# A decoder layer on one core: the FFN's out-projection as seven block products, with sums of operands formed on the fly

## The chip, the cores and the metric

One Trainium2 chip; the program runs on one core. The metric is the device time of one execution in microseconds (us), lower is better. A time is the median of several executions; beside it stands one profiled execution with its trace. The engines are called by the profile's names: PE (TensorE, matrix products), PEld (its weight loads), DVE (VectorE), ACT (ScalarE), POOL (GpSimd) and SP (SyncE, which only issues DMA transfers here).

## The reference

One layer over 1024 tokens of width 1024, all in fp32 (DEPTH is 1, so the sparse-attention branch is never reached):

```
def swiglu(x, w_in, w_out):
    a, b = jnp.split(x @ w_in, 2, axis=-1)
    return (jax.nn.silu(a) * b) @ w_out

h = x
h = h + stick_breaking_attention(rms_norm(h, norm_mix), w_in, w_out)   # 16 heads of 64
h = h + swiglu(rms_norm(h, norm_ffn), ffn_w_in, ffn_w_out)             # inner width 2816
gate = sigmoid(rms_norm(h, norm_ple) @ ple_w_gate)
h = h + gate * (p @ ple_w_proj)                                        # p: 1024 x 256
return rms_norm(h, final_norm)
```

## The kernel before

**Precision.** Each fp32 operand is split into a high part (a cast to fp32r, by ACT) and a low part (operand minus high part, by DVE or POOL). A product of two operands is then three matmuls: high by high, high by low, low by high (`mm3`, L126 to L129). Every matmul spoken of here has a 128x128 weight tile and 512 columns.

**Layout.** Tensors lie transposed: features on the 128 partitions, tokens along the free dimension. Width 1024 is 8 tiles (KT), the inner width 2816 is 22 tiles (NFF), and the tokens are taken in two halves of 512 (h).

**Stages.** Start (the first norm's split of x, its square sums, first Q and K products), attention with its projections (heads in pairs, 8 pairs), the embedding projection `p @ ple_w_proj` in the midst of that (stored to memory as `ple`, for the end), attention's out-projection, the FFN's in-projection, the FFN's out-projection, the gate with the final norm. Up to the FFN a scheduler orders the instructions; from the in-projection on, each engine runs in the order in which the code is written.

**FFN in-projection.** For each of the 22 inner tiles the 2x2-block product is computed with seven block products in place of eight (products P1 to P7 by Winograd's variant of Strassen's scheme; sums of weight blocks are formed by DVE, split by ACT and DVE or POOL). The SwiGLU result of tile k goes to memory as `act_d[k][h]`. The last tile's scalings are kept back as `rest_0` and `rest_1`, four DVE operations and one of ACT each, and are called inside the out-projection.

**FFN out-projection.** For h in 0, 1 and for k in 0 to 21: load `act_d[k][h]` (L618, 256 KB) and split it (`act_split`; ACT L626, DVE L627), load weight tile `w_fo[k]` (512 KB) and split it (`w_split`; ACT L106, DVE L108), then 8 output tiles m, three matmuls each, into 8 PSUM banks. That is 2 x 22 x 8 x 3 = 1056 matmuls. The last two k are done per m, so that the banks finish one by one; `residual` (L939) then adds h from memory. In the second half `parts3(m, 0)` splits the finished first half for the gate (ACT L944 `gh`, DVE L945 `gl`, ACT L950 square, and a sum of squares on POOL or DVE, L952). Five gate weights are split between k = 3 and k = 18 (`WGK`).

**Start.** Zeros for the unused halves of K's tiles (`KLS`) are written by POOL from a tile `zero` that POOL has set itself; the tile is also the source of ACT's `pad`.

**Embedding projection.** Each 128x512 block is copied from PSUM by ACT to a tile `plt` (three buffers in rotation, tag `qf`) and stored, 16 stores of 256 KB.

Of the kernel before, what the change touches and what calls it, by code (L numbers as in the profile page):

```python
# [40 lines left out]
def tile_trunk(ctx: ExitStack, tc: tile.TileContext, xT, pT, gains, ident, w_qkv, w_o, w_fi, w_fo, w_g, w_p, outT):  # L41
# [22 lines left out]
    for m in MORD:  # L64
        order.append((w_o[m], KT))
    n_fi = len(order)
    for h in range(2):
        for k in range(NFF):
            order.append((w_fo[k], KT, k == NFF - 1))
            if h == 1 and k in WGK:  # L70
                order.append((w_g[WGK.index(k)], KT, True))
    for m in range(len(WGK), KT):
        order.append((w_g[m], KT, m < 6))

    N1 = 3 * NPAIR + 2
    raws, parts, loaded = {}, {}, set()
# [19 lines left out]
    def w_split(k):  # L96
        if k < lim[0] and k in raws:
            n = order[k][1]
            t = raws.pop(k)
            if len(order[k]) > 2 and order[k][2]:  # L100
                hi = xp.tile([P, T], F32R, name=f"whi{k}", tag="X").rearrange("p (k m) -> p k m", k=KT)
                lo = xp.tile([P, T], F32R, name=f"wlo{k}", tag="X").rearrange("p (k m) -> p k m", k=KT)
            else:
                hi = wp.tile([P, KT, P], F32R, name=f"whi{k}", tag="whi", bufs=2)
                lo = wp.tile([P, KT, P], F32R, name=f"wlo{k}", tag="wlo", bufs=2)
            nc.scalar.copy(hi[:, :n, :], t[:, :n, :])  # L106
            eng = nc.gpsimd if k < N1 or n_fi <= k < n_fi + 2 or k >= len(order) - 3 else nc.vector
# [61 lines left out]
    with ExitStack() as c1:  # L169
# [77 lines left out]
        for kt in range(KT):  # L247
# [240 lines left out]
        def ple_steps():  # L488
# [118 lines left out]
    def tmp(name):  # L607
        return pt.tile([P, 512], F32, name=name, tag="t")

    ring[:] = [0, ctx.enter_context(tc.tile_pool(name="pr", bufs=2, reuse_waits="tile"))]  # L610

    tc_manual = tc.manual_schedule()
    acts = {}
    araw = {}

    def act_dma(i):
        if i < 2 * NFF and i not in araw and i not in acts:
            h, k = divmod(i, NFF)  # L618
            araw[i] = tmp("araw")
            nc.sync.dma_start(araw[i], act_d[k][h])  # L620

    def act_split(i):
        if i < 2 * NFF and i not in acts:
            t = araw.pop(i)
            a = duo(xp, f"act{i}", "X", None)
            nc.scalar.copy(a[:, 0, :], t)  # L626
            nc.vector.tensor_tensor(a[:, 1, :], t, f(a[:, 0, :]), op=ALU.subtract)  # L627
            acts[i] = a

    with ExitStack() as c2:  # L630
        p2 = c2.enter_context(tc.tile_pool(name="p2", bufs=1, reuse_waits="tile"))

        def add(out, x, y):
            nc.vector.tensor_tensor(out, x, y, op=ALU.add)  # L634
# [208 lines left out]
        for k in range(NFF):  # L843
            w = wc
            wc, todo = fi_prep(k + 1)
            fi_load(k + 2)
            if k >= NFF - 2:
                for i in range(2):
                    w_load(n_fi + 2 * (k + 2 - NFF) + i)
                act_dma(k + 2 - NFF)  # L850
            ps1 = prod(w["A11"], "B11")
            q1 = tmp("q1")
            nc.scalar.copy(q1, ps1)
# [41 lines left out]
            todo[4]()  # L895
            if 0 < k < NFF - 1:
                glu(k, 0, q1, u2)
            if k == NFF - 1:
                act_dma(2)
            ps3 = prod(w["S4"], "B22")  # L900
            if k == 0:
                for h in range(2):
# [20 lines left out]
            glu(NFF - 1, 1, u4, c22)  # L923

        rests = [rest_0, rest_1]


    p3 = ctx.enter_context(tc.tile_pool(name="p3", bufs=1, reuse_waits="tile"))
    hres = [p3.tile([P, T], F32, name=f"h{m}") for m in range(KT)]
    hh = [p3.tile([P, T], F32R, name=f"gh{m}") for m in range(KT)]  # L930
    hl = [p3.tile([P, T], F32R, name=f"gl{m}") for m in range(KT)]
# [6 lines left out]
    def residual(m, h, ps, t):  # L938
        nc.vector.tensor_tensor(hres[m][:, HS[h]], ps, t, op=ALU.add)  # L939

    def parts3(m, h):
        hs = HS[h]
        g = gn[:, 2, m:m + 1]
        nc.scalar.activation(hh[m][:, hs], hres[m][:, hs], AF.Copy, scale=g)  # L944
        nc.vector.scalar_tensor_tensor(hl[m][:, hs], hres[m][:, hs], g, f(hh[m][:, hs]), op0=ALU.mult, op1=ALU.subtract)  # L945
        if m == 0:
            nc.scalar.activation(acc3[:, hs], hres[m][:, hs], AF.Square)
        else:
            s = tmp("sq")
            nc.scalar.activation(s, hres[m][:, hs], AF.Square)  # L950
            eng = nc.vector if h and m % 2 else nc.gpsimd
            eng.tensor_tensor(acc3[:, hs], acc3[:, hs], s, op=ALU.add)  # L952

    y3 = None
    for h in range(2):
        pm = [None] * KT
        tail = []
        for k in range(NFF):
            i = h * NFF + k
            act_dma(i)  # L960
            act_split(i)
            act_dma(i + 1)
            act_dma(i + 2)
            wh, wl = w_next()
            if h == 1 and 2 <= k < 10:
                parts3(k - 2, 0)
            act_split(i + 1)
            a = acts.pop(i)
            if h == 1 and k in WGK:
                wg.append(w_next())  # L970
            if k < NFF - 2:
                for m in range(KT):
                    if k == 0:
                        pm[m] = mb()
                    mm3(pm[m], wh[:, m, :], wl[:, m, :], a[:, 0, :], a[:, 1, :], k == 0, False)
            else:
                tail.append((wh, wl, a))
            if k and rests:
                rests.pop(0)()
        res = []  # L980
        for m in range(KT):
            t = tmp("h2")
            nc.sync.dma_start(t, h2_d[m][h])
            res.append(t)
        for m in range(KT):
            for q, (wh, wl, a) in enumerate(tail):
                mm3(pm[m], wh[:, m, :], wl[:, m, :], a[:, 0, :], a[:, 1, :], False, q == 1)
            residual(m, h, pm[m], res[m])


    acc4 = row("acc4")
# [50 lines left out]
    for ri, (c0, n) in enumerate(ranges):  # L1042
# [3 lines left out]
        for m in range(KT):  # L1046
# [81 lines left out]
```

## Time and profile before

| what | value |
|---|---|
| median of 3 runs | 1380.06 us (1379.49 to 1381.41) |
| profiled execution: its own time | 1380.04 us |
| profiled execution: span of the trace | 1378.3 us |
| granted TensorE clock, mean | 0.996 |
| PE busy | 1353.9 us (98%) |
| DVE busy | 1004.1 us (73%) |
| ACT busy | 607.6 us (44%) |
| POOL busy | 408.3 us (30%) |

The span runs from the first to the last instruction in the trace; the execution's own time is 1.7 us longer. Busy shares are means over stages that are limited by different things. A matmul of 512 columns shows as 0.39 us, but the next begins 0.23 us later: matmuls overlap, and their rate is read from their starts.

### The profile page before, as it was taken

The numbers are of one execution on the slowest core, as the hardware profiler recorded it, in microseconds if no ns is written. First come the engines' busy times: TensorE is split into PE (matmuls) and PEld (weight loads), VectorE is DVE, ScalarE is ACT, GpSimd is POOL, SyncE is SP. The second block draws the span as 40 slices with busy tenths as digits, with TensorE's granted clock in tenths as the row PEclk, the third lists the DMA queues.
The fourth block names the chain that finished last, engine by engine and source line by source line (L and its number), as shares of the span: only waits on it lengthen the run. The fifth ranks groups of instructions, "written<-read, shape, count | busy, mean of one in ns | idle before, by whom it ended". The sixth has DMA issues, their size and how long they took to land. (4 is left out here: it accounts for less than half of the span.)

```text
span 1378.3 us, 17601 instructions
## 1 busy us (share of the span) xinstructions
PE 1353.9 (98%) x6620; PEld 1133.0 (82%) x6620; DVE 1004.1 (73%) x1305; ACT 607.6 (44%) x1082; POOL 408.3 (30%) x280
## 2 busy tenths in 40 slices
PE   8999999999999999999999999999999999999996
PEld 6888888888888888888888888888888888888896
DVE  6878878787887866677878888888884335635675
ACT  6555565656556665443222223222323233534322
POOL 2222221313222401245454544545450000301321
PEclk9999999999999999999999999999999999999998
DMA  5101111110101662442221222212235446455123
GB/s 185 62 16 61 31 48 45 47 47 31 61 31 68 208 237 70 148 143 78 92 92 63 75 92 92 92 62 76 92 138 183 138 143 227 150 181 178 35 72 101
DMA packets 55509, 137.54 MB, mean 100 GB/s; under 512 B 6016, under 2 KB 10496, under 8 KB 55424
## 3 DMA queue, kind: packets, MB, share of 16 engines
q1 hardware_dynamic: 53136, 128.82, 27.2%
q0 software_dynamic: 2016, 7.34, 1.5%
q8 instruction: 52, 0.85, 0.2%
q14 instruction: 33, 0.27, 0.1%
q10 hardware_dynamic: 272, 0.26, 0.1%
HBM read 104.94 MB, written 31.46 MB: 99 GB/s over the span
## 5 line engine op out<-in xcount | busy, mean ns | idle before, releaser
L417 DVE TENSOR_TENSOR_SCAN a<-a,hot 128x128 f32<-128x128 f32 (+7 forms) x128 | 188.8, 1491 | 24.6 <-ACT a L410 24.0
L108 POOL TENSOR_TENSOR wlo<-wraw,whi 128x1024 fp32r<-128x1024 f32 x29 | 72.8, 2516 | 293.3 <-ACT whi L106 117.9
L106 ACT CAST whi<-wraw 128x1024 fp32r<-128x1024 f32 x84 | 88.2, 1051 | 161.8 <-PE b_m L128 144.6
L108 DVE TENSOR_TENSOR wlo<-wraw,whi 128x1024 fp32r<-128x1024 f32 x55 | 69.1, 1257 | 119.6 <-ACT whi L106 119.5
L127 PE MATMUL b_pj<-xh,whi 128*128 128x512 f32 x352 | 140.6, 399 | 0.0
L129 PE MATMUL b_pj<-xh,wlo 128*128 128x512 f32 x352 | 138.7, 394 | 0.4 <-POOL wlo L108 0.4
L128 PE MATMUL b_pj<-xl,whi 128*128 128x512 f32 x352 | 137.8, 391 | 0.0
L440 DVE TENSOR_TENSOR al<-b_tp,ah 128x512 fp32r<-128x512 f32 (+2 forms) x160 | 93.1, 599 | 53.9 <-ACT ah L439 53.5
L439 ACT CAST ah<-b_tp 128x512 fp32r<-128x512 f32 (+2 forms) x160 | 82.0, 522 | 78.7 <-PE b_tp L430 77.8
L410 ACT ACTIVATE a<-b_z 128x128 f32<-128x128 f32 (+2 forms) x192 | 87.0, 491 | 49.0 <-PE b_z L408 47.8
L128 PE MATMUL b_m<-act,whi 128*128 128x512 f32 x264 | 102.8, 389 | 0.4 <-DVE act L627 0.4
L127 PE MATMUL b_m<-act,whi 128*128 128x512 f32 x264 | 102.8, 389 | 0.0
L129 PE MATMUL b_m<-act,wlo 128*128 128x512 f32 x264 | 102.7, 389 | 0.0
L430 PE MATMUL b_tp<-hot,a 128*128 128x128 f32 x576 | 94.3, 273 | 2.5 <-DVE al L440 2.5
L430 PEld LDWEIGHTS b_tp<-hot,a 128*128 128x128 f32 x576 | 72.6, 140 | 25.8 <-DVE al L440 5.5
L129 PEld LDWEIGHTS b_pj<-xh,wlo 128*128 128x128 f32 x352 | 66.0, 188 | 16.2 <-POOL wlo L108 0.5
L128 PEld LDWEIGHTS b_pj<-xl,whi 128*128 128x128 f32 x352 | 66.2, 188 | 8.9
L127 PEld LDWEIGHTS b_pj<-xh,whi 128*128 128x128 f32 x352 | 66.1, 188 | 8.6
L450 PE MATMUL b_av<-ah,V 128*128 128x512 f32 (+2 forms) x160 | 70.7, 442 | 0.0
L952 POOL TENSOR_TENSOR acc<-acc,sq 128x512 f32<-128x512 f32 x10 | 17.6, 1756 | 158.5 <-ACT sq L950 157.8
L832 ACT ACTIVATE sg<-u 128x512 f32<-128x512 f32 x22 | 13.9, 633 | 108.8 <-issue 86.6
L128 PEld LDWEIGHTS b_m<-act,whi 128*128 128x128 f32 x264 | 49.6, 188 | 11.1 <-DVE act L627 0.8
(3040 smaller groups left out, 3745.6 us busy)
## 6 DMA issues: line engine op xcount, KB each, us to landing
fraw<-w_fi SPq DMA_DIRECT2D x44, 512.0 KB, 4.4
wraw<-w_fo SPq DMA_DIRECT2D x44, 512.0 KB, 3.7
wraw<-w_qkv SPq DMA_DIRECT2D x22, 512.0 KB, 3.6
araw<-act SPq DMA_DIRECT2D x44, 256.0 KB, 3.9
h<-h SPq DMA_DIRECT2D x32, 256.0 KB, 3.1
sp<-hl SPq DMA_DIRECT2D x14, 512.0 KB, 3.0
act<-u SPq DMA_DIRECT2D x22, 256.0 KB, 2.2
act<-c SPq DMA_DIRECT2D x22, 256.0 KB, 2.6
```

The costliest lines, as they stand in the source:

```text
L106: nc.scalar.copy(hi[:, :n, :], t[:, :n, :])
L108: eng.tensor_tensor(lo[:, :n, :], t[:, :n, :], f(hi[:, :n, :]), op=ALU.subtract)
L127: nc.tensor.matmul(ps, whi, xhi, start=first, stop=False)
L128: nc.tensor.matmul(ps, whi, xlo, start=False, stop=False)
L129: nc.tensor.matmul(ps, wlo, xhi, start=False, stop=last)
L410: nc.scalar.activation(a[:, c0:c0 + e], z[:, :e], AF.Sigmoid, scale=-SCALE)
L417: nc.vector.tensor_tensor_scan(a[:, L - 1::-1], a[:, L - 1::-1], hot[:, back], 0.0, op0=ALU.mult, op1=ALU.max)
L430: nc.tensor.transpose(b[:, j * P:(j + 1) * P], a[:, kt * P:(kt + 1) * P], idn)
L439: nc.scalar.copy(ah[:, m0:m0 + 512 - j0 * P], b[:, j0 * P:])
L440: nc.vector.tensor_tensor(al[:, m0:m0 + 512 - j0 * P], b[:, j0 * P:], f(ah[:, m0:m0 + 512 - j0 * P]), op=ALU.subtract)
L450: nc.tensor.matmul(ps[:, c0:], o.V[:, kt, hd, :], ah[:, r0:], start=kt == 0, stop=False)
L952: eng.tensor_tensor(acc3[:, hs], acc3[:, hs], s, op=ALU.add)
```

## The change

**Out-projection.** The product is cut into 2x2 blocks: the inner width into two halves c of 11 tiles (tile j + 11c), the output width into two halves r of 4 tiles, the tokens into two halves h. It is computed as seven block products in the order P1, P5, P6, P7, P2, P4, P3 (`FO`). Each takes 11 steps (j) of 4 output tiles x 3 matmuls, so 77 steps of 12 matmuls, 924 in all. Weight block and activation block of a step lie side by side in one 128x1024 tile `[w | x]`. P1 and P2 take plain blocks (`SX` and `raw` hold them). P5, P6 and P7 take differences or sums: `SX[j]` becomes the pair's difference in place (L652, DVE, 128x1024), then `d - SX[j]`, then a sum in the load's own tile. P4 needs a difference for its activation half alone, P3 for its weight half alone (L652, 128x512). The high part of the pair is one ACT cast of 128x1024 (L672), the low part one DVE subtraction of 128x1024 (L684); for P1 both are done in two halves (L670, L682).

In the loop over the steps n, code order is: load for n + 6, low part for n + 2 (`fo_lo`), then sum and high part for n + 3 (`fo_hi`), gate weights where due, the 12 matmuls, and up to two jobs from a list. Jobs add a finished product to the outputs (`evac_fo`: P1 and P5 an ACT copy each, P6, P2, P4 and P3 one DVE addition for each of the 4 tiles, P7 three) and, in P4 and P3, `parts3(m, 0)`. The residual h comes by POOL's DMA that adds into the tile. Five gate weights are split within P2.

**Start.** `zero` is set by DVE in place of POOL, PE runs 9 matmuls of 128 columns on it ahead of everything, and the zero fills of K's tiles stand later in the code.

**Embedding projection.** `plt` takes 1024 columns in the Q and K tags (KA, KB, QA, QB; two buffers each), with 8 stores of 512 KB.

```
+        nc.vector.memset(zero, 0.0)
...
-        nc.gpsimd.memset(zero, 0.0)
+        busy = jb()
+        for _ in range(9):
+            nc.tensor.matmul(busy[:, :P], zero, zero, start=True, stop=True)
...
-                                t = p1.tile([P, 512], F32, name="plt", tag="qf", bufs=3)
-                                nc.scalar.copy(t, ps)
-                                nc.sync.dma_start(ple_d[m4 * 4 + m][:, hs], t)
+                                if h == 0:
+                                    t = p1.tile([P, T], F32, name="plt", tag=("KA", "KB", "QA", "QB")[m], bufs=2)
+                                nc.scalar.copy(t[:, hs], ps)
+                                if h:
+                                    nc.sync.dma_start(ple_d[m4 * 4 + m], t)
...
+    FO = ("P1", "P5", "P6", "P7", "P2", "P4", "P3")
+    NJ = NFF // 2
+    NS = len(FO) * NJ
...
+    def fo_hi(n):
...
+        if p == "P5":
+            tt(SX[j], SX[j], d)
+            d = SX[j]
+        elif p == "P6":
+            tt(SX[j], d, SX[j])
+            d = SX[j]
+        elif p == "P7":
+            tt(d, d, SX[j], ALU.add)
+        elif p == "P4":
+            tt(d[:, 1, :], d[:, 1, :], SX[j][:, 1, :])
+        elif p == "P3":
+            tt(SX[j][:, 0, :], d[0], SX[j][:, 0, :])
+            d = SX[j]
+        hi = duo(xp, f"fh{n}", "X", None)
...
+            nc.scalar.copy(hi, d)
+        fop[n] = d, hi
+
+    def fo_lo(n):
...
+            nc.vector.tensor_tensor(lo, d, f(hi), op=ALU.subtract)
+        fop[n] = hi, lo
...
-    for h in range(2):
-        pm = [None] * KT
-        tail = []
-        for k in range(NFF):
...
+    for n in (3, 4, 5):
+        fo_load(n)
+    fo_hi(2)
+    for n in range(NS):
+        p, j = FO[n // NJ], n % NJ
+        fo_load(n + 6)
+        if n < 3:
+            nc.sync.dma_start(SX[n][:, 1, :], act_d[n][0])
+        if 5 <= n < 5 + NJ:
+            fo_w(SX[n - 5][:, 0, :], n - 5, 1, 1)
+        fo_lo(n + 2)
+        fo_hi(n + 3)
+        if (p, j) in gate_split:
+            w_split(n_fi + gate_split[(p, j)])
...
+        hi, lo = fop.pop(n)
+        for i in range(4):
+            ws = slice(i * P, i * P + P)
+            mm3(pm[i], hi[:, 0, ws], lo[:, 0, ws], hi[:, 1, :], lo[:, 1, :], j == 0, j == NJ - 1)
+        if n in (2, 5):
+            rests.pop(0)()
+        if j == NJ - 1:
+            jobs += [lambda p=p, i=i, ps=ps: evac_fo(p, i, ps) for i, ps in enumerate(pm)]
+            more = {"P2": range(4), "P4": range(4, KT)}
+            jobs += [lambda m=m: parts3(m, 0) for m in more.get(p, ())]
+        elif j:
+            left = NJ - 1 - j
+            for _ in range(1 if len(jobs) <= left else 2):
+                if jobs:
+                    jobs.pop(0)()
```

**How it moves the instructions.** In the kernel before, DVE's queue in the out-projection holds the low parts of weights (`wlo`, L108) and activations (`act`, L627) in turn; each reads a load and ACT's high part of that load:

```order
L108 TENSOR_TENSOR wlo_9595<-wraw_9508,whi_9594 128x1024
L627 TENSOR_TENSOR act_9598<-araw,act_9598 128x512
L108 TENSOR_TENSOR wlo_9630<-wraw_9550,whi_9629 128x1024
L627 TENSOR_TENSOR act_9633<-araw,act_9633 128x512
L108 TENSOR_TENSOR wlo_9665<-wraw_9592,whi_9664 128x1024
```

In the changed kernel the same queue, at the passage from P1 to P5, reads as follows. `s` is `SX`, `fh` and `fl` are the high and low part of a step:

```order
L682 TENSOR_TENSOR fl_9668<-raw_9570,fh_9649 128x512
L682 TENSOR_TENSOR fl_9668<-s_9453,fh_9649 128x512
L652 TENSOR_TENSOR s_9438<-s_9438,raw_9591 128x1024
L684 TENSOR_TENSOR fl_9690<-s_9438,fh_9672 128x1024
L652 TENSOR_TENSOR s_9445<-s_9445,raw_9620 128x1024
L684 TENSOR_TENSOR fl_9711<-s_9445,fh_9693 128x1024
L652 TENSOR_TENSOR s_9452<-s_9452,raw_9642 128x1024
L684 TENSOR_TENSOR fl_9732<-s_9452,fh_9714 128x1024
```

A pair's difference (L652) is now followed directly by the low part of that same pair (L684), which reads the high part that ACT makes of the difference in between. ACT's queue at this place holds those casts, one behind the other:

```order
L670 CAST fh_9649<-s_9453 128x512
L672 CAST fh_9672<-s_9438 128x1024
L672 CAST fh_9693<-s_9445 128x1024
L672 CAST fh_9714<-s_9452 128x1024
L672 CAST fh_9735<-s_9459 128x1024
L672 CAST fh_9760<-s_9441 128x1024
```

At the passage from P4 to P3 DVE's queue holds the half-size differences, and between them and the low parts the gate's splits (`g_0`, L1023) and sums of squares (`acc`, L1031):

```order
L652 TENSOR_TENSOR raw_10758<-raw_10758,s_9456 128x512
L1023 SCALAR_TENSOR_TENSOR g_0_10844<-h_9447,gn,g_0_10844 128x512
L1031 TENSOR_TENSOR acc_9463<-acc_9463,sq 128x512
L684 TENSOR_TENSOR fl_10853<-raw_10758,fh_10830 128x1024
L652 TENSOR_TENSOR raw_10779<-raw_10779,s_9453 128x512
L1023 SCALAR_TENSOR_TENSOR g_0_10870<-h_9454,gn,g_0_10870 128x512
L684 TENSOR_TENSOR fl_10879<-raw_10779,fh_10856 128x1024
L652 TENSOR_TENSOR s_9438<-fw,s_9438 128x512
```

POOL's queue at the start of the program keeps its order in the changed kernel, but for `zero`, which is no longer in it; the fills of K's tiles (`KLA`, `KLB`, L261) still come first of its longer work:

```order
L198 MEMSET hot 128x896
L199 MEMSET ones 128x1
L212 MEMSET vf_142 128x1
L212 MEMSET vf_143 128x1
L261 CAST KLA_146<-zero 64x1024
L261 CAST KLB_147<-zero 64x1024
L261 CAST KLA_148<-zero 64x1024
```

Only the place in the code has moved; in the queue the fills stand where they stood.

## Rows read from the trace of the kernel before

**Rows 1.** The page: span, busy time of PE and DVE, share, instructions.

```profile
span 1378.3 us, 17601 instructions
...
PE 1353.9 (98%) x6620; PEld 1133.0 (82%) x6620; DVE 1004.1 (73%) x1305; ACT 607.6 (44%) x1082; POOL 408.3 (30%) x280
```

**Rows 2.** Busy time by windows: one of the out-projection, one at the end.

```profile
core 0: us, PE busy (x) PEld busy (x) DVE busy (x) ACT busy (x) POOL busy (x), PEclk, DMA share, GB/s
1100.00:1200.00 100.00, 100.00 (x443) 82.81 (x442) 52.30 (x54) 40.04 (x55) 11.02 (x6) 1.00 0.52 176
...
1360.00:1370.00 10.00, 4.87 (x36) 4.52 (x35) 5.74 (x21) 2.66 (x7) 0.68 (x1) 0.84 0.24 80
```

**Rows 3.** Timeline of PE: start us, us, matmul; out-projection's first, gate's first.

```profile
1028.54 0.39 PE L127 MATMUL b_m<-act,whi 128*128 128x512 f32 x1
...
1268.77 0.39 PE L127 MATMUL b_m<-gh,whi 128*128 128x512 f32 x1
```

**Rows 4.** Groups by form, out-projection: busy us, mean ns, idle before and releaser.

```profile
L108 DVE TENSOR_TENSOR wlo<-wraw,whi 128x1024 fp32r<-128x1024 f32 x47 | 57.5, 1223 | 114.4 <-ACT whi L106 114.3
L106 ACT CAST whi<-wraw 128x1024 fp32r<-128x1024 f32 x50 | 52.6, 1054 | 151.3 <-PE b_m L128 144.6 <-issue 3.9 <-PE b_m L129 2.6
...
L944 ACT ACTIVATE gh<-h,gn 128x512 fp32r<-128x512 f32 x8 | 5.8, 722 | 0.0
```

**Rows 5.** Timelines of ACT and DVE: a high part, its low part, the first rest.

```profile
1034.86 1.05 ACT L106 CAST whi<-wraw 128x1024 fp32r<-128x1024 f32 x1 [5.04 <-PE b_m L128]
1035.82 0.61 ACT L626 CAST act<-araw 128x512 fp32r<-128x512 f32 x1
...
1035.95 1.23 DVE L108 TENSOR_TENSOR wlo<-wraw,whi 128x1024 fp32r<-128x1024 f32 x1 [2.61 <-ACT whi L106]
1037.09 0.69 DVE L627 TENSOR_TENSOR act<-araw,act 128x512 fp32r<-128x512 f32 x1
1037.69 0.69 DVE L828 TENSOR_TENSOR q<-q,rstd 128x512 f32<-128x512 f32 x1
...
1039.81 0.69 DVE L834 TENSOR_TENSOR u<-q,u 128x512 f32<-128x512 f32 x1
```

**Rows 6.** Timelines of DVE and ACT, in-projection: sum, its high part, its low part.

```profile
912.89 0.69 DVE L637 TENSOR_TENSOR s<-s,fraw 128x512 f32<-128x512 f32 x1
914.26 1.01 DVE L689 TENSOR_TENSOR wc16S<-s,wc16S 128x512 fp32r<-128x512 f32 x1 [0.69 <-ACT wc16S L686]
...
913.61 0.62 ACT L686 CAST wc16S<-s 128x512 fp32r<-128x512 f32 x1 [0.58 <-DVE s L637]
```

**Rows 7.** Timelines of DVE and ACT at the in-projection's end: an activation after DVE.

```profile
1023.57 0.69 DVE L828 TENSOR_TENSOR u<-u,rstd 128x512 f32<-128x512 f32 x1
...
1024.36 0.63 ACT L832 ACTIVATE sg<-u 128x512 f32<-128x512 f32 x1 [5.09 <-DVE u L828]
```

**Rows 8.** Timelines of DVE and POOL, while both work on square sums.

```profile
1164.78 0.75 DVE L945 SCALAR_TENSOR_TENSOR gl<-h,gn,gh 128x512 fp32r<-128x512 f32 x1
1165.44 1.79 DVE L627 TENSOR_TENSOR act<-araw,act 128x512 fp32r<-128x512 f32 x1
...
1164.82 1.85 POOL L952 TENSOR_TENSOR acc<-acc,sq 128x512 f32<-128x512 f32 x1 [133.31 <-ACT sq L950]
```

**Rows 9.** Timelines of PE and DVE at the start of the program.

```profile
10.43 0.63 PE L128 MATMUL b_av<-xl,whi_s 128*128 128x512 f32 x1
10.86 0.63 PE L129 MATMUL b_av<-xh,wlo_s 128*128 128x512 f32 x1
...
15.86 0.50 PE L128 MATMUL b_z<-xl,whi_s 128*128 128x512 f32 x1 [0.33 <-DVE xl L239]
...
15.73 1.22 DVE L245 TENSOR_TENSOR acc<-acc,sq 128x1024 f32<-128x1024 f32 x1
```

**Rows 10.** Timeline of PE in the embedding projection.

```profile
491.13 0.50 PE L127 MATMUL b_pj<-ph,whi 128*128 128x512 f32 x1 [1.36 <-ACT plt L513]
```

**Rows 11.** DMA issues of the whole run: size, median us to landing.

```profile
wraw<-w_fo SPq DMA_DIRECT2D x44, 512.0 KB, 3.7
```

More of the change, by code (lines that the diff above doesn't have):

```diff
@@ L66, in tile_trunk @@
     n_fi = len(order)
-    for h in range(2):
-        for k in range(NFF):
[L69 to L73, printed above, removed]
+    for m in range(KT):
+        order.append((w_g[m], KT, m > 1))
     N1 = 3 * NPAIR + 2
@@ L265, in tile_trunk @@
         x_square(KT - 1)
+        for q in range(2):
+            for hd in range(2):
+                r = slice(64 - 64 * hd, 128 - 64 * hd)
+                nc.gpsimd.tensor_copy(KLS[q][hd][r, :], zero[r, 0:1].to_broadcast([64, T]))
         cur[0] = 2
@@ new lines, in fo_hi, with tt @@
+    def fo_hi(n):
+        if n >= NS:
+            return
+        p, j = FO[n // NJ], n % NJ
+        d = fraw.pop(n)
+        def tt(out, a, b, op=ALU.subtract):
+            nc.vector.tensor_tensor(out, a, b, op=op)
+        if p == "P5":
[8 more added lines that the diff above has]
+            tt(d[:, 1, :], d[:, 1, :], SX[j][:, 1, :])
+        elif p == "P3":
+            tt(SX[j][:, 0, :], d[0], SX[j][:, 0, :])
+            d = SX[j]
+        hi = duo(xp, f"fh{n}", "X", None)
+        if p == "P1":
+            for q in range(2):
+                nc.scalar.copy(hi[:, q, :], d[q])
+        else:
+            nc.scalar.copy(hi, d)
+        fop[n] = d, hi
@@ L630, in tile_trunk, with fo_prep @@
+    def fo_lo(n):
+        if n >= NS:
+            return
+        d, hi = fop[n]
+        lo = duo(xp, f"fl{n}", "X", None)
+        if isinstance(d, tuple):
+            for q in range(2):
+                nc.vector.tensor_tensor(lo[:, q, :], d[q], f(hi[:, q, :]), op=ALU.subtract)
+        else:
+            nc.vector.tensor_tensor(lo, d, f(hi), op=ALU.subtract)
+        fop[n] = hi, lo
+    def fo_prep(n):
+        fo_hi(n)
+        fo_lo(n)
     with ExitStack() as c2:
         p2 = c2.enter_context(tc.tile_pool(name="p2", bufs=1, reuse_waits="tile"))
+        ring[:] = [0, c2.enter_context(tc.tile_pool(name="pr", bufs=2, reuse_waits="tile"))]
@@ L846, in tile_trunk @@
             fi_load(k + 2)
[L847 to L850, printed above, removed]
+            if k == NFF - 1:
+                for n in range(3):
+                    fo_load(n)
             ps1 = prod(w["A11"], "B11")
@@ L936, in tile_trunk, with gx @@
     nc.vector.tensor_scalar(gf, gn[:, 3, :], RF, None, op0=ALU.mult)
[L938 to L939 removed]
+    def gx(kt, c0, n):
+        h = c0 // 512
+        cs = slice(c0 - 512 * h, c0 - 512 * h + n)
+        return hh[h][kt][:, cs], hl[h][kt][:, cs]
+    begun = set()
     def parts3(m, h):
@@ L950, in parts3 @@
             nc.scalar.activation(s, hres[m][:, hs], AF.Square)
-            eng = nc.vector if h and m % 2 else nc.gpsimd
+            eng = nc.vector if m % 2 else nc.gpsimd
             eng.tensor_tensor(acc3[:, hs], acc3[:, hs], s, op=ALU.add)
-    y3 = None
-    for h in range(2):
-        pm = [None] * KT
-        tail = []
[L958 to L988, printed above, removed]
@@ new lines, in plus, with residual, evac_fo @@
+    def plus(out, x, y, op=ALU.add):
+        nc.vector.tensor_tensor(out, x, y, op=op)
+    def residual(m, h):
+        nc.gpsimd.dma_start(hres[m][:, HS[h]], h2_d[m][h], accum_op=ALU.add)
+    def evac_fo(p, i, ps):
+        c11, c12 = hres[i][:, HS[0]], hres[i][:, HS[1]]
+        c21, c22 = hres[i + 4][:, HS[0]], hres[i + 4][:, HS[1]]
+        if p == "P1":
+            nc.scalar.copy(c11, ps)
+        elif p == "P5":
+            nc.scalar.copy(c22, ps)
+        elif p == "P6":
+            plus(c21, ps, c11)
+            residual(i, 0)
+        elif p == "P7":
+            plus(c12, c21, c22, ALU.subtract)
+            residual(i, 1)
+            plus(c21, ps, c21, ALU.subtract)
+            plus(c22, c21, c22)
+            residual(i + 4, 1)
+            residual(i + 4, 0)
+        elif p == "P2":
+            plus(c11, ps, c11)
+        elif p == "P4":
+            plus(c21, ps, c21)
+        else:
+            plus(c12, ps, c12)
@@ new lines, in tile_trunk @@
+    gate_load = {("P6", 8): 0, ("P7", 4): 1, ("P2", 1): 2, ("P2", 3): 3, ("P2", 5): 4, ("P4", 1): 5, ("P4", 2): 6}
+    gate_split = {("P2", 1): 0, ("P2", 3): 1, ("P2", 5): 2, ("P2", 7): 3, ("P2", 9): 4}
+    n_wg = len(gate_split)
+    jobs = []
+    for n in (3, 4, 5):
+        fo_load(n)
+    fo_hi(2)
+    for n in range(NS):
+        p, j = FO[n // NJ], n % NJ
+        fo_load(n + 6)
+        if n < 3:
+            nc.sync.dma_start(SX[n][:, 1, :], act_d[n][0])
[5 more added lines that the diff above has]
+            w_split(n_fi + gate_split[(p, j)])
+        if (p, j) in gate_load:
+            w_load(n_fi + gate_load[(p, j)])
+        if j == 0:
+            pm = [mb() for _ in range(4)]
+        hi, lo = fop.pop(n)
[13 more added lines that the diff above has]
+                    jobs.pop(0)()
@@ L991, in tile_trunk @@
+    while jobs:
+        jobs.pop(0)()
+    for q in range(n_wg):
+        wg.append(parts.pop(n_fi + q))
+    cur[0] = n_fi + n_wg
     acc4 = row("acc4")
```

87 lines of the change are left out of this document (51 added, 36 removed).

## The prediction

> **What bounds the kernel now.** The page comes first: PE is busy in 98% of the span, DVE in 73% [rows 1]. So a saving counts where PE has fewer matmuls to do, as long as PE is still fed. The windows say the same of the stage that is rewritten: between 1100 and 1200 us PE is busy without a gap at the full clock, DVE for 52.3 us, ACT for 40.0 us, and the DMA engines for half the time at 176 GB/s [rows 2]. The timeline gives the stage's length: its first matmul starts at 1028.54 us, the gate's first at 1268.77 us [rows 3]. That is 240.2 us for 1056 matmuls, 0.2275 us for one, as they follow each other. The groups by form show who waits for whom: DVE's low parts of weights idle 114 us ahead of ACT's high parts, and these 145 us for PE to free a slot [rows 4]. Preparation runs ahead and is held back by PE.
>
> **The sum that the change invites.** 77 steps of 12 matmuls are 924, 132 fewer: 132 x 0.2275 = 30.0 us. A step takes PE 12 x 0.2275 = 2.73 us. What has to be asked is whether DVE and ACT can prepare a step in that time.
>
> **Work of DVE by step.** A low part of a 128x1024 pair takes 1.14 us from start to start (1035.95 to 1037.09) [rows 5]. A sum of two such tiles shows as 1.22 us [rows 9]. So for P5, P6 and P7 DVE works 1.22 + 1.14 = 2.36 us in a step, under PE's 2.73 us. By busy time it would do.
>
> **The order in DVE's queue.** It is not busy time that decides. In the changed queue the low part stands directly behind the difference of the same pair, and reads the high part that ACT casts from that difference. DVE takes its queue in order, so it stands still while ACT casts. The next difference can't start until that low part is done. Nothing stands between them in P5 and P6; in P7, P4 and P3 a job's addition does, which fits into the wait. A step is a chain:
> - difference 1.22 us [rows 9];
> - handover to ACT: 0.03 us in the nearest case (912.89 + 0.69 to 913.61 [rows 6]), 0.10 us where ACT waited for more (1023.57 + 0.69 to 1024.36 [rows 7]). I take 0.09, since this cast also needs a free slot;
> - cast of 128x1024: 1.05 us [rows 4];
> - handover to DVE 0.03 us (913.61 + 0.62 to 914.26 [rows 6]);
> - low part 1.14 us.
>
> Together 3.53 us. With 0.03 for the first handover it is 3.47, with 0.10 and the low part at its shown 1.22 us [rows 4] it is 3.62. Rows 6 is the same pattern at half the size: sum, cast, low part, with DVE standing still for 0.69 us; there other work hides it, here it comes every step. PE needs 2.73 us for a step, so PE waits 0.8 us in each once its lead is used up.
>
> **The sum along DVE's queue**, from the end of the last in-projection matmul to that of the out-projection:
> - Up to the first difference: 0.9 us for the in-projection's last addition (0.69 and a handover of 0.1 on either side), nine low parts in two halves, 9 x 1.2 = 10.8 us (halves start 0.6 us apart: 1037.09 to 1037.69), and two rests of 2.81 us (1037.69 to 1040.50) [rows 5]: 17.3 us. PE comes to that step only at 11 x 2.73 = 30.0 us; the lead is used up in P5 to P7. Could loads be later? Up to there they move 9 x 0.52 + 4 x 0.26 = 5.8 MB. The window moves 176 GB/s at a share of 0.52 [rows 2], so 338 GB/s in full: 17.1 us, and 3.7 us to land [rows 11], 20.8 us if the first of them goes out at zero. Bounds 17.3 and 20.8; I take 17.3, as the first loads go out before zero.
> - P5, P6, P7: 33 x 3.53 = 116.5 us (114.5 to 119.5).
> - P2 has no sums. ACT casts straight from loads and runs ahead. DVE: 11 low parts and four gate weights' (each a 128x1024 subtraction as well), 15 x 1.14 = 17.1 us, and P7's four jobs of three additions of 0.69, 8.3 us: 25.4 us. PE catches up its backlog here.
> - P4 and P3, 22 steps: the difference is of one half, 0.69 us [rows 5], so the chain is 0.69 + 0.10 + 1.05 + 0.03 + 1.14 = 3.01 us. Fifteen of them are 45.1 us. In seven, a `parts3` stands between difference and low part: ACT scales (`gh`, 0.72 us [rows 4], starting 0.96 behind the cast [rows 5]), then DVE makes `gl`, 0.75 us [rows 8]: 0.69 + 0.10 + 0.96 + 0.72 + 0.03 + 0.75 + 1.14 = 4.39 us. For m = 1, 3, 5 DVE also adds a square, 0.60: 4.99. For m = 2, 4, 6 POOL adds it, and beside POOL's addition a DVE subtraction took 1.79 us where it takes 0.69 [rows 8, 5]: 4.39 + 1.1 = 5.49. (m = 7 comes behind the last low part.) 4.39 + 3 x 4.99 + 3 x 5.49 = 35.8 us.
> - PE's last step behind its low part: 2.8 us.
>
> 17.3 + 116.5 + 25.4 + 45.1 + 35.8 + 2.8 = 242.9 us, against 240.2 before: 2.7 us longer. With all handovers and loads at their lower ends, and POOL's additions costing nothing, it is 237; at the upper ends 249. The 30.0 us that PE saves are given back as its waits.
>
> **The other edits.** The embedding tiles: PE waited once for ACT's copy there, 1.36 us [rows 10]; ACT was held by the store of an earlier `plt`. Eight tiles in place of three take that wait away: -1.4 us. Below nothing it isn't, since the tags used are free by then. **The warm-up**: matmuls on zeros could raise the granted clock earlier, and the starts there are 0.43 us apart (10.43 to 10.86) against 0.2275 later. But at 15.86 us PE waits for DVE's split of x (`xl`) [rows 9], whatever its clock was, and DVE is fed by x's arrival: 0. If it did count, 12 matmuls at 0.2 us, 2.4 us, are its upper end. **Zero fills later**: POOL's queue shows the same order, so they run at the same time: 0. **Behind the out-projection** nothing changes: the gate has the same matmuls and splits.
>
> The sum is made against the profiled execution, 1380.04 us, 0.02 under the median: 1380.04 + 2.7 - 1.4 = 1381.3, about 1381 us. A measurement can hardly tell less than 0.2% (2.8 us) from no change: faster is under 1377.3, slower over 1382.8.
>
> **Rivals.**
> - *PE sets the pace, DVE's waits are hidden.* This needs a low part that doesn't wait for its own cast, or a cast of about 0.2 us. For it: DVE's and ACT's busy time fit. Against it: the queue's order, and rows 6. Then 1380.04 - 30.0 - 1.4 = 1348.6 us. Chance 0.08.
> - *The start of the chain is late, and it ends slower.* Place: P1. The loads of steps 9 and on stand in SP's queue behind the store of `rest_0`, which waits for DVE. If that store goes out 3 us later than I reckon (0.9, three low parts and a rest, 7.3 us), loads instead of DVE set the first difference, at 20.8 us or later. Everything behind it is one chain, so the delay counts in full: 1385 at 20.8, 1389 if P4's loads, whose ring has three slots, stall too. It decides from a delay of 1.5 us on. Chance 0.15.
> - *The clock falls.* PE now waits 0.8 us in every 3.5. The granted clock was 1.00 while PE was busy throughout and 0.84 between 1360 and 1370, where PE was busy for 4.87 us of 10, with waits in between [rows 2]. At the lower of the two levels, 1.2 GHz, the starts are 0.43 us apart [rows 9] and a step takes 12 x 0.43 = 5.2 us, which is over the chain's 3.53: PE would set the pace. If it held in half of the 33 steps, 16 x 1.65 = 27 us: about 1408. Against it: a slowed PE has no waits any more. Chance 0.05. The Trainium skill says of this ("TensorE: Matmul & The Clock Gate", section "A second HAM failure mode: psum-queue depth-cycling") that a TensorE which idles briefly between groups of matmuls can swing between the two levels and lose throughput in swinging. By that page this rival would be the likeliest, at about 1408; no stretch of this trace has such waits in a row, so no row decides it.
>
> **Chances and range.** The chain as reckoned has 0.72, and within it 1375 to 1389 by its bounds: 0.12 of that under 1377.3, 0.35 between the limits, 0.25 over. With the rivals: faster 0.12 + 0.08 = 0.20; same 0.35; slower 0.25 + 0.15 + 0.05 = 0.45. From 1374 to 1391 us the range holds the chain and most of the late start, a little over 8 in 10; the hidden chain and the fallen clock lie outside it.
>
> **What would show it.** PE's busy time in the stage about 210 us of 243, with waits of about 0.8 us ahead of the first matmul that reads a low part, released by DVE's L684. DVE's L684 idle about 1.1 us each in P5 to P7, released by ACT's L672, starts of L652 3.5 us apart there and 3.0 us in P4 and P3. No wait in P2, none for loads. The embedding's wait gone, the start the same within 0.5 us. The forecast is wrong if L684 starts without idle time, if the starts of L652 are 2.7 us apart, or if PE's releaser there is a DMA.

## The result, and the profile after

| what | before | after |
|---|---|---|
| median | 1379.86 us (4 runs) | 1392.26 us (1390.67 to 1394.17, 4 runs) |
| span of the profiled execution | 1378.3 us | 1389.9 us |
| PE busy | 1353.9 us, 6620 matmuls | 1343.3 us, 6506 matmuls |
| first matmul of the out-projection | 1028.54 us | 1025.32 us |
| first matmul of the gate | 1268.77 us | 1281.12 us |

The changed kernel is slower: ratio 1.0087, 95% interval 1.0073 to 1.0100. The median is 11 us over the forecast and 1.3 us over the range's upper end.

The table's last two rows divide the difference of 11.6 us between the spans. The out-projection starts 3.2 us earlier, takes 255.8 us where it took 240.2, and what follows takes 0.7 us less: -3.2 + 15.6 - 0.7 = 11.7. So PE has 132 matmuls of 512 columns less to do in the stage, and the stage is 15.6 us longer. (The table counts 114 less: the nine matmuls of the warm-up stand in the trace as 18 records.)

DVE's timeline of the changed kernel, at the passage from P1 to P5 (start, duration, engine, line, operation; in brackets the idle time before it and who ended it):

```profile
1044.98 0.69 DVE L682 TENSOR_TENSOR fl<-s,fh 128x512 fp32r<-128x512 f32 x1
1045.59 1.22 DVE L652 TENSOR_TENSOR s<-s,raw 128x1024 f32<-128x1024 f32 x1
1048.05 1.23 DVE L684 TENSOR_TENSOR fl<-s,fh 128x1024 fp32r<-128x1024 f32 x1 [1.25 <-ACT fh L672]
1049.19 1.22 DVE L652 TENSOR_TENSOR s<-s,raw 128x1024 f32<-128x1024 f32 x1
1051.58 1.23 DVE L684 TENSOR_TENSOR fl<-s,fh 128x1024 fp32r<-128x1024 f32 x1 [1.16 <-ACT fh L672]
```

Each low part waits 1.2 us for the cast of its own pair; from one difference to the next it is 3.60 us here, and 117.5 us for all 33 steps of P5 to P7 (1045.59 to 1163.08), 3.56 each. Groups of the stage (busy us, mean ns, then the idle time before them and who ended it) and waits (us in total, times, longest) show whom this holds up:

```profile
L684 DVE TENSOR_TENSOR fl<-s,fh 128x1024 fp32r<-128x1024 f32 x33 | 42.6, 1290 | 32.1 <-ACT fh L672 32.1
L684 DVE TENSOR_TENSOR fl<-raw,fh 128x1024 fp32r<-128x1024 f32 x33 | 41.0, 1255 | 17.2 <-ACT fh L672 17.2
...
PE b_pj L120 <- DVE fl L684: 15.3, 18, 2.8
PE b_m L120 <- DVE fl L684: 11.0, 15, 2.3
```

Before the change, DVE and ACT waited for PE [rows 4]; now DVE waits 49.3 us for ACT, and PE 26.3 us in 33 waits for DVE. PE's timeline shows the pace (matmuls that read a low part, once the lead is used up):

```profile
1127.23 0.50 PE L120 MATMUL b_pj<-fl,fh 128*128 128x512 f32 x1 [0.51 <-DVE fl L684]
1130.84 0.50 PE L120 MATMUL b_pj<-fl,fh 128*128 128x512 f32 x1 [0.59 <-DVE fl L684]
```

They stand 3.61 us apart where 12 matmuls take 2.73. The wait shows as 0.5 to 0.6 us, not 0.8, since a matmul is drawn longer than the distance to the next.

**Where it is longer than reckoned.** DVE's timeline at the end of the in-projection, whose last matmul precedes 1025.32:

```profile
1025.57 0.69 DVE L696 TENSOR_TENSOR c<-b_m,u 128x512 f32<-128x512 f32 x1
1026.18 0.68 DVE L696 TENSOR_TENSOR q<-b_m,q 128x512 f32<-128x512 f32 x1
1026.78 0.68 DVE L682 TENSOR_TENSOR fl<-fw,fh 128x512 fp32r<-128x512 f32 x1
1027.38 0.69 DVE L682 TENSOR_TENSOR fl<-fx,fh 128x512 fp32r<-128x512 f32 x1
1027.98 1.28 DVE L696 TENSOR_TENSOR u<-b_m,u 128x512 f32<-128x512 f32 x2
```

DVE is free not 0.9 us behind PE but 3.9 us (its next operation starts at 1029.18): it has the additions of earlier products and the low part of step 1 still to do. So the first difference starts at 20.3 us, not 17.3.

The second place is the passage from P2 to P4, in the timelines of ACT (the first two lines) and DVE:

```profile
1187.99 1.05 ACT L672 CAST fh<-raw 128x1024 fp32r<-128x1024 f32 x1 [7.25 <-DMA raw<-act]
1188.94 1.05 ACT L100 CAST whi<-wraw 128x1024 fp32r<-128x1024 f32 x1
...
1190.03 1.23 DVE L102 TENSOR_TENSOR wlo<-wraw,whi 128x1024 fp32r<-128x1024 f32 x1 [3.58 <-ACT whi L100]
1191.17 1.22 DVE L684 TENSOR_TENSOR fl<-raw,fh 128x1024 fp32r<-128x1024 f32 x1
1192.30 0.69 DVE L652 TENSOR_TENSOR raw<-raw,s 128x512 f32<-128x512 f32 x1
1194.23 1.23 DVE L684 TENSOR_TENSOR fl<-raw,fh 128x1024 fp32r<-128x1024 f32 x1 [1.25 <-ACT fh L672]
1198.52 0.69 DVE L652 TENSOR_TENSOR raw<-raw,s 128x512 f32<-128x512 f32 x1 [3.06 <-DMA raw<-act]
1201.32 1.23 DVE L102 TENSOR_TENSOR wlo<-wraw,whi 128x1024 fp32r<-128x1024 f32 x1 [2.10 <-ACT whi L100]
1202.46 1.22 DVE L684 TENSOR_TENSOR fl<-raw,fh 128x1024 fp32r<-128x1024 f32 x1
1203.60 0.69 DVE L652 TENSOR_TENSOR raw<-raw,s 128x512 f32<-128x512 f32 x1
```

P2 lasts 29.2 us on DVE (1163.08 to 1192.30; reckoned 25.4), and the first two steps of P4 11.3 us (1192.30 to 1203.60; reckoned 6.0). Besides the chain's own 1.25 us, DVE has three waits there. The 3.06 us are for a load. The 3.58 us are a load's doing as well: DVE waits for ACT's cast of a gate weight, which stands in ACT's queue behind a cast that waited 7.25 us for its load. The 2.10 us are the fifth gate weight's. The windows (busy times of PE, PEld, DVE, ACT and POOL, granted clock, DMA share, GB/s) and the DMA issues between 1163 and 1192 us say why loads are late (the last two lines: packets, MB and share of the 16 DMA engines by queue; q1 is SP's, q0 POOL's):

```profile
1090.00:1163.00 73.00, 61.95 (x247) 44.37 (x245) 50.69 (x45) 24.71 (x27) 3.55 (x4) 1.00 0.58 173
1176.00:1180.00 4.00, 4.00 (x19) 3.30 (x19) 3.86 (x6) 2.31 (x3) 2.26 (x4) 1.00 1.12 250
1184.00:1188.00 4.00, 4.00 (x19) 3.34 (x18) 2.44 (x3) 0.01 (x1) 0.54 (x1) 1.00 1.11 262
1200.00:1204.00 4.00, 0.77 (x2) 0.46 (x3) 2.68 (x3) 1.28 (x2) 0.00 (x0) 0.81 0.26 98
1204.00:1208.00 4.00, 4.00 (x10) 3.13 (x11) 2.11 (x3) 1.53 (x2) 0.00 (x0) 0.50 0.41 140
...
h<-h POOLq DMA_DIRECT2D x12, 256.0 KB, 12.1
raw<-w_fo SPq DMA_DIRECT2D x8, 256.0 KB, 8.2
raw<-act SPq DMA_DIRECT2D x8, 256.0 KB, 9.7
wraw<-w_g SPq DMA_DIRECT2D x3, 512.0 KB, 7.3
...
q1 hardware_dynamic: 2077, 4.45, 49.3%
q0 software_dynamic: 1254, 2.30, 43.3%
```

From 1176 us on the DMA engines are full, with twelve transfers of h that add into the output (P7's jobs) beside the loads. A load of an activation takes 9.7 us to land, where it took 3.1 in P6 and P7.

The rest of P4 and P3 is as reckoned: 86.1 us from 1192.30 to the end of the last low part at 1278.43, less the 5.3 us of the first two steps, is 80.8 against 80.9.

### The profile page after: what moved, and what is told of

It reads as the page before. It is cut to its first block, busy times and chain, and to the rows that moved or that the text cites. A ratio compares the mean times of both kernels' runs of the same rounds, so it can differ in the third digit from the quotient of the medians.

```text
span 1389.9 us, 17597 instructions
## 1 busy us (share of the span) xinstructions
PE 1343.3 (97%) x6506; PEld 1112.2 (80%) x6506; DVE 1076.6 (77%) x1379; ACT 626.3 (45%) x1091; POOL 408.8 (29%) x289
## 5 line engine op out<-in xcount | busy, mean ns | idle before, releaser
L413 DVE TENSOR_TENSOR_SCAN a<-a,hot 128x128 f32<-128x128 f32 (+7 forms) x128 | 193.1, 1524 | 21.9 <-ACT a L406 21.5
L102 POOL TENSOR_TENSOR wlo<-wraw,whi 128x1024 fp32r<-128x1024 f32 x27 | 67.5, 2501 | 225.5 <-ACT whi L100 130.5
L120 PE MATMUL b_m<-fl,fh 128*128 128x512 f32 x231 | 94.0, 407 | 11.2 <-DVE fl L684 11.0
L121 PE MATMUL b_m<-fh,fl 128*128 128x512 f32 x231 | 91.8, 397 | 0.0
L119 PE MATMUL b_m<-fh 128*128 128x512 f32 x231 | 91.8, 397 | 0.0
L672 ACT CAST fh<-s 128x1024 fp32r<-128x1024 f32 x33 | 34.7, 1050 | 78.2 <-DVE s L652 65.8
L120 PEld LDWEIGHTS b_m<-fl,fh 128*128 128x128 f32 x231 | 44.2, 191 | 29.8 <-DVE fl L684 20.7
L684 DVE TENSOR_TENSOR fl<-s,fh 128x1024 fp32r<-128x1024 f32 x33 | 42.6, 1290 | 32.1 <-ACT fh L672 32.1
L672 ACT CAST fh<-raw 128x1024 fp32r<-128x1024 f32 x33 | 34.0, 1049 | 69.6 <-DVE raw L652 56.1
```

The source lines that it names most:

```text
L119: nc.tensor.matmul(ps, whi, xhi, start=first, stop=False)
L120: nc.tensor.matmul(ps, whi, xlo, start=False, stop=False)
L121: nc.tensor.matmul(ps, wlo, xhi, start=False, stop=last)
L413: nc.vector.tensor_tensor_scan(a[:, L - 1::-1], a[:, L - 1::-1], hot[:, back], 0.0, op0=ALU.mult, op1=ALU.max)
L672: nc.scalar.copy(hi, d)
L684: nc.vector.tensor_tensor(lo, d, f(hi), op=ALU.subtract)
```

## The experiments

The comparisons are with runs of the kernel before on the same chip (medians 1379.9 to 1380.6 us). "Stage" is from the first matmul of the out-projection to the gate's first.

### e1: the sum of a step ahead of the low part of the step before

```
-        fo_lo(n + 2)
         fo_hi(n + 3)
+        fo_lo(n + 2)
```

> The changed kernel with one thing altered: in each step the sum and high part for n + 3 are issued ahead of the low part for n + 2, so that DVE has the low part of the step before to do while ACT casts. Same work, same loads. Chain theory (DVE's queue order sets the pace of P5 to P7, P4 and P3): starts of L652 are paced by PE at 2.73 us in P5 to P7 in place of 3.55, DVE's waits for ACT's L672 nearly vanish (49 us before), the stage falls from 255.8 to 211 to 218 us, so the time is 1347 to 1356 us. Load theory (late loads of P2 and P4 set it, and PE would be late at the same places): P2 and the first steps of P4 still lose about 9 us and little else changes: 1380 to 1392 us.

Measured: 1351.68 us (1351.18 to 1352.47), ratio to before 0.9790 (0.9773 to 0.9806); stage 214.5 us. The same work, two lines exchanged, is 40.6 us faster than the changed kernel. DVE's timeline of this run has no wait between the operations:

```profile
1053.20 1.22 DVE L652 TENSOR_TENSOR s<-s,raw 128x1024 f32<-128x1024 f32 x1
1054.34 1.22 DVE L684 TENSOR_TENSOR fl<-s,fh 128x1024 fp32r<-128x1024 f32 x1
1055.47 1.22 DVE L652 TENSOR_TENSOR s<-s,raw 128x1024 f32<-128x1024 f32 x1
```

One step takes DVE 2.27 us until PE holds it back. The chain theory holds: by the load theory the time would have stayed at 1380 to 1392.

### e2: gate weights through POOL's DMA queue

```
-            nc.sync.dma_start(t[:, :n, :], src)
+            (nc.gpsimd if k >= n_fi else nc.sync).dma_start(t[:, :n, :], src)
```

> The changed kernel with the gate's weights loaded through POOL's DMA queue in place of SP's, nothing else altered. The after trace shows SP standing 14.3 us in three waits of a gate weight's load for its buffer, with the loads for P2 and P4 behind it, and DVE and ACT then waiting for those loads. If that is the cause of the two longer terms (P2 29.2 us where 25.4 was reckoned, and 5.3 us more in the first two steps of P4), these waits go and the time falls by 5 to 9 us, to 1383 to 1387 us; the chain's 3.55 us a step in P5 to P7 stays. If the chain alone sets the time, or the loads are slow for another reason (their rate), it stays at 1392 us within 1.5.

Measured: 1391.95 us (1390.93 to 1393.65); stage 256.3 us. The forecast gain of 5 to 9 us is missing. The timelines of ACT and DVE show what took the place of the waits for loads:

```profile
1188.54 1.05 ACT L100 CAST whi<-wraw 128x1024 fp32r<-128x1024 f32 x1 [8.39 <-DMA wraw<-w_g]
...
1201.52 1.22 DVE L102 TENSOR_TENSOR wlo<-wraw,whi 128x1024 fp32r<-128x1024 f32 x1 [5.87 <-ACT whi L100]
```

The gate's weight itself was late now, and ACT's queue stood behind it. P2 is shorter, 26.8 us on DVE (1165.07 to 1191.89) against 29.2, but P4's first two steps take 11.9 us in place of 11.3: the fifth gate weight makes DVE wait 5.87 us there. The run doesn't tell the order of SP's queue from the crowd of transfers, since POOL's queue also carries the twelve transfers of h. The gate weights took 10.4 us to land in it between 1163 and 1192 us, against 7.3 through SP's, and the loads that stayed with SP 5.4 and 6.1 us, against 8.2 and 9.7.

### e3: casts and low parts in halves

```
-            nc.scalar.copy(hi, d)
+        for q in range(2):
+            nc.scalar.copy(hi[:, q, :], d[q] if p == "P1" else d[:, q, :])
...
-            nc.vector.tensor_tensor(lo, d, f(hi), op=ALU.subtract)
+        for q in range(2):
+            s = d[q] if isinstance(d, tuple) else d[:, q, :]
+            nc.vector.tensor_tensor(lo[:, q, :], s, f(hi[:, q, :]), op=ALU.subtract)
```

> The changed kernel with every cast of a high part and every subtraction of a low part made in two halves of 512 columns, order otherwise the same. More instructions, the same work. Chain theory: the second half's cast runs while DVE does the first half's low part, so a step in P5 to P7 is 1.22 + 0.09 + 0.62 + 0.03 + 1.20 = 3.16 us where 3.55 was measured, 12 to 13 us less over 33 steps, and about 3 us less each in P4 and P3: 1373 to 1378 us. If DVE's or ACT's throughput or the loads set the pace, two instructions for one can only cost: 1392 us or more.

Measured: 1374.53 us (1373.38 to 1374.93), ratio 0.9955 (0.9940 to 0.9970); stage 238.5 us. DVE's timeline:

```profile
1048.88 1.22 DVE L652 TENSOR_TENSOR s<-s,raw 128x1024 f32<-128x1024 f32 x1
1050.83 1.29 DVE L679 TENSOR_TENSOR fl<-s,fh 128x512 fp32r<-128x512 f32 x2 [0.73 <-ACT fh L669]
1052.05 1.21 DVE L652 TENSOR_TENSOR s<-s,raw 128x1024 f32<-128x1024 f32 x1
```

A step is 3.17 us, the reckoned 3.16, with one more instruction on each engine. The time follows the length of the chain, not the amount of work.

### e4: e1 and e2 together

> Both of the alterations before together: sums ahead of the low part of the step before, and gate weights through POOL's DMA queue. Chain theory with late loads as a second, smaller term: PE sets the pace throughout, the stage is 211 to 214 us, the time 1346 to 1352 us, and the gain over the order alone is under 5 us, since DVE then has a lead of several steps that covers most of the late loads. If loads set the time once the chain is gone, this is at least 7 us faster than the order alone.

Measured: 1352.41 us (1352.12 to 1352.73); stage 214.8 us, as in e1. The time is 0.4 us over the expected range; as expected, nothing is left for the loads' queue to give.

### e5: without the twelve transfers of h that P7 issues

```
             plus(c12, c21, c22, ALU.subtract)
-            residual(i, 1)
             plus(c21, ps, c21, ALU.subtract)
             plus(c22, c21, c22)
-            residual(i + 4, 1)
-            residual(i + 4, 0)
```

> The changed kernel without the twelve transfers that P7's jobs issue on POOL to add h into three quarters of the output (the output lacks h there); the other four and all else stay. The trace of the changed kernel shows the DMA engines full from about 1172 to 1200 us, when these twelve move beside the loads: a load takes 8 to 10 us to land where it takes 3 elsewhere. If these transfers, and not the order of SP's queue, make P2's and P4's loads late, P2 falls from 29.2 to about 25.4 us on DVE's queue and P4's first two steps from 11.3 to about 6, so the time is 1381 to 1386 us; the 3.5 us steps of P5 to P7 stay. If they are not the cause, 1390 to 1393 us.

Measured: 1384.99 us (1384.77 to 1387.37), 7.3 us under the changed kernel. The DMA issues of the same 29 us:

```profile
raw<-w_fo SPq DMA_DIRECT2D x8, 256.0 KB, 4.3
raw<-act SPq DMA_DIRECT2D x8, 256.0 KB, 4.6
wraw<-w_g SPq DMA_DIRECT2D x3, 512.0 KB, 3.6
```

and DVE's timeline at the start of P4:

```profile
1189.54 0.68 DVE L652 TENSOR_TENSOR raw<-raw,s 128x512 f32<-128x512 f32 x1
...
1195.40 1.22 DVE L102 TENSOR_TENSOR wlo<-wraw,whi 128x1024 fp32r<-128x1024 f32 x1 [2.11 <-ACT whi L100]
...
1197.68 0.68 DVE L652 TENSOR_TENSOR raw<-raw,s 128x512 f32<-128x512 f32 x1
```

P2 is 25.5 us on DVE (1163.99 to 1189.54) where 25.4 was reckoned, and DVE's wait for a load is gone. SP's own waits for a gate weight's buffer, which e2 was meant to remove, are still there (waits: us in total, times, longest; 14.3 us in the changed kernel):

```profile
SPq L87 <- DVE wlo L102: 13.5, 3, 5.3
```

So without the crowd of transfers that order of SP's queue costs DVE nothing in P2; with them, the loads land too late. The crowd is what makes these two excesses. P4's first two steps still take 8.1 us, not 6.0: the fifth gate weight's low part stands between a difference and its low part, and waits 2.1 us for a cast that ACT does behind the pair's.

### e6 and e7: the kernel before with one of the small edits

e6 has the embedding edit alone, e7 the start's edits alone, as in the diff.

> The kernel before with the embedding edit alone (1024 columns in the free Q and K buffers, 8 stores). The prediction's term is 1.4 us, the one wait that PE shows. Between the two traces PE's matmuls move ahead by 2.35 us from about 440 us to the FFN's start, 1 us more. If all of that is this edit's, the time falls by 2.0 to 2.4 us; if the rest comes from the reordering that the start's edit causes, by 1.4.

Measured: 1377.81 us (10 runs, 1376.07 to 1380.08), ratio 0.9981 (0.9971 to 0.9990), 2.6 us, a little more than expected. In the trace PE's matmuls gain 2.4 us on those of before between 440 us and the end of this stage. PE's own wait was 1.36 us [rows 10]; its weight load waited 1.8 us at the same place, and 1.6 us of the gain come there. The other 0.75 us come between 473 and 478 us; which wait they were is not shown.

> The kernel before with the start's edits alone: zeros set by DVE, nine matmuls on zeros ahead of x, zero fills later in the code. The prediction's term is 0. PE's matmuls stand 0.6 us earlier after the start and 0.9 us earlier by 300 us in the trace of the changed kernel. If the start's edits do this, the time falls by 0.6 to 0.9 us, which is less than the interval of the comparison; the place of PE's matmuls in the trace will tell.

Measured: 1380.96 us (10 runs, 1378.71 to 1383.29), ratio 1.0004 (0.9994 to 1.0014): no change. The early gain of 1.2 us that its trace shows against that of before is lost again at the embedding tiles, where PE's waits grow from 1.4 to 2.4 us. In e6, whose start is unchanged, PE also stands 0.7 us ahead there, so that much differs between executions.

### e8: eight of the twelve transfers written later

```
             plus(c12, c21, c22, ALU.subtract)
-            residual(i, 1)
             plus(c21, ps, c21, ALU.subtract)
             plus(c22, c21, c22)
-            residual(i + 4, 1)
             residual(i + 4, 0)
         elif p == "P2":
             plus(c11, ps, c11)
+            residual(i + 4, 1)
         elif p == "P4":
             plus(c21, ps, c21)
+            residual(i, 1)
```

> The changed kernel with eight of the twelve transfers of h issued later: four with the jobs of P2 (which run in P4), four with the jobs of P4 (which run in P3); all the work is kept. If the crowd of transfers is what delays the loads, most of what leaving them out gives is kept: 1383 to 1388 us. If their total counts and not their time, 1390 to 1393 us.

Measured: 1390.09 us (1388.55 to 1390.64), 2.2 us under the changed kernel; the time decides little, for only four of the eight went out later. POOL's timeline shows the other four in a row behind P7's last:

```profile
1183.78 4.51 POOL L1037 DMA_DIRECT2D h<-h  x5 [2.60 <-DVE h L1034]
1232.74 1.27 POOL L1031 TENSOR_TENSOR acc<-acc,sq 128x512 f32<-128x512 f32 x1 [44.45 <-ACT sq L1029]
1233.96 3.58 POOL L1037 DMA_DIRECT2D h<-h  x4
```

POOL had nothing to wait for, so the later place in the code didn't hold them. The last four stood behind a sum that waits for P4's jobs. What the four in a row did shows in DVE's timeline at the start of P4:

```profile
1189.99 0.68 DVE L652 TENSOR_TENSOR raw<-raw,s 128x512 f32<-128x512 f32 x1
...
1197.07 0.69 DVE L652 TENSOR_TENSOR raw<-raw,s 128x512 f32<-128x512 f32 x1 [3.92 <-DMA raw<-act]
```

P2 is back at 25.5 us on DVE (1164.44 to 1189.99), as without the twelve, and P4's first two steps take 12.2 us (to 1202.15) in place of 11.3. The wait moved with the transfers, which speaks for their place rather than their total.

### e9: the order of e1 for P5 to P7 only

```
+        if n + 3 < 5 * NJ:
+            fo_hi(n + 3)
+            fo_lo(n + 2)
+        else:
+            fo_lo(n + 2)
+            fo_hi(n + 3)
```

> The changed kernel with the order altered (sums ahead of the low part of the step before) for P5, P6 and P7 only; P4 and P3 keep the changed kernel's order. Chain theory, in numbers: with the order altered throughout, DVE reaches P4's first sum at 1165.7 us; P4 and P3 took DVE 86.1 us in the changed kernel's order and PE 2.8 us more behind the last low part, so the out-projection ends at 1254.6 us in place of 1241.0: 13.6 us slower than with the order altered throughout, 1365 us (1361 to 1368). If PE's lead at P4's start covers the shorter chain of 3.0 us a step, or if only the sums of two halves matter: 1351 to 1354 us.

Measured: 1366.03 us (1364.50 to 1368.00), ratio 0.9899 (0.9884 to 0.9914); the gate's first matmul at 1255.25 us, where 1254.6 was reckoned. So P4 and P3 were a chain of their own: P5 to P7's order gives 26 us and P4 and P3's 14.

### e10: e1 with the transfers of e8

> The order altered throughout, and eight of P7's twelve transfers of h written with the jobs of P2 and P4 (of which only the last four went out later when this was tried on the changed kernel). PE waits only 3.1 us in the whole stage with the order altered, so this can give at most that: 1349 to 1352 us. If the crowd of transfers still costs its 7.3 us once the chain is gone, 1346 us or less.

Measured: 1349.34 us (1348.45 to 1351.33), ratio 0.9782 (0.9766 to 0.9798), the fastest version; 2.3 us under e1, but the two intervals overlap. Stage 212.4 us, against 924 x 0.2275 = 210.2 for the matmuls alone; PE's waits in it fall from 3.1 to 2.1 us. The crowd of transfers, worth 7.3 us in the changed kernel, is nearly covered by the lead that DVE has here.

## Why the prediction was wrong, by its steps

The mechanism, a chain through DVE's queue that gives back what PE saves, was right. What failed is the stretch that was to be free of it: "No wait in P2, none for loads". There 7.0 us came from loads that landed late beside twelve transfers that the prediction didn't count, and 2.1 us from a gate weight that it didn't count. Ahead of it 3.0 us came from a start of the chain that was put too early.

- **The chain DVE, ACT, DVE in P5 to P7: right.** 116.5 us were reckoned, 117.5 measured; e1 takes it away, e3 shortens it by the reckoned amount. By e9 the order costs 26 us in P5 to P7 and 14 in P4 and P3, more than the 30 us that PE saves.
- **P4 and P3: right in mechanism and size**, 80.9 reckoned and 80.8 measured without the excess of the first two steps; POOL's sums cost what rows 8 show (a low part of 2.29 us where it takes 1.22). That the two agree to 0.1 us is in part luck: of the later twenty steps, the 13 plain ones took 39.5 us where 39.1 was reckoned, and the seven with a `parts3` 35.4 where 35.8 was. e9 isolates this part.
- **"0.9 us for the in-projection's last addition": too small by 3.0 us.** DVE was 3.9 us behind PE there. Since everything behind the first difference is one chain, this counts in full.
- **"P2 has no sums. ACT casts straight from loads and runs ahead": failed, 3.8 us.** ACT didn't run ahead, as the loads were late. The prediction counted P7's additions on DVE and left out the twelve transfers that the same jobs issue on POOL. e5 shows them as the cause. PE, which had a backlog, waited for nothing in P2; DVE's delay reached it in P4, in waits of 1.7 and 2.8 us.
- **P4's first steps: 5.3 us too short.** 3.2 us are a late load of the same cause, 2.1 the fifth gate weight, which was not counted at all.
- **The late start as a rival**: its condition came true, for the store of `rest_0` went out at 10.4 us (1035.69) where 7.3 was reckoned. What it was to cause did not: DVE waited for no load up to the first difference, which came at 20.3 us by DVE's own additions. For P4's loads the rival named SP's queue; what the runs show as the cause there is the crowd of transfers. Whether taking away SP's waits alone would have done as well stays open, since e2 put the gate weights into the crowd's queue.
- **The small edits**: embedding 2.6 us in e6 against 1.4; start 0 as reckoned. The zero fills were not tried alone; e7 has them with the rest.
- **The falling clock**: not in P5 to P7, where the granted clock is 1.00 in spite of 0.5 us waits in every step. The Trainium skill's account of a TensorE that idles briefly between groups of matmuls and swings between the two levels ("TensorE: Matmul & The Clock Gate", section "A second HAM failure mode: psum-queue depth-cycling") doesn't describe this stretch. In P4 and P3 the granted clock did fall in places, behind longer waits, but DVE's chain went on setting the pace (80.8 us against 80.9).

Together: 3.0 + 1.0 + 3.8 + 5.3 = 13.1 us more in the stage; 12.9 were measured (255.8 against 242.9), as P4 and P3's rest and PE's last step were 0.1 us shorter each. Against that, the stage began 3.2 us earlier where 1.4 was forecast, and what follows it took 0.7 us less: 1381.3 + 12.9 - 1.8 - 0.7 = 1391.7, and the profiled execution took 1391.86. Of the 3.2 us, 2.35 are gained at the embedding tiles and 0.9 before them; e6, whose start is that of before, is 0.7 us ahead there too, so this is no effect of the start's edits that a run shows. The gate's 0.7 us are not explained.

## What to carry to other kernels

When an operation is fed by a sum that has to be formed first, look in the in-order queue of the engine that does both: if the consumer stands directly behind its own producer with another engine's step between, the step costs the sum of the three operations, whatever the busy time says. One step of software pipelining more, two lines exchanged, was worth 40 us here and turned a loss of 0.9% into a gain of 2.1%. And count every transfer that a moved job issues: where they came in a bunch here, ordinary loads took about twice as long to land (8.2 and 9.7 us, against 4.3 and 4.6 without them).

## What the runs showed that was not expected

The clock fell where the waits were few and longer. Behind PE's waits of 1.7 and 2.8 us at 1200 us the window 1204 to 1208 is at 0.50 of full speed (1.2 GHz), with 10 matmuls in 4 us; behind waits of 1.95 and 2.4 us the window 1236 to 1240 is at 0.58 in the mean, and behind waits of 2.3 and 1.8 us the window 1272 to 1276 at 0.77. The 0.5 us waits in every step of P5 to P7 left it at 1.00.

The transfers that add into their target were dear for the DMA engines: between 1163 and 1192 us they moved 2.30 MB in 43.3% of the 16 engines' time, SP's plain loads 4.45 MB in 49.3%, so a MB of them took about 1.7 times as long (an estimate from these shares). Whether the adding or the queue makes them so is not shown.
